# One PSUM tile shared out by the program, and seven column products in another order

## The chip, the cores and the metric

The kernel runs on one core of one Trainium2 chip. TensorE (PE in the profile, its weight loads PEld) multiplies, VectorE is DVE, ScalarE is ACT, GpSimd is POOL, and SyncE (SP) issues most DMAs. The metric is device time in microseconds (us) of one execution.

## The reference, cut to what matters

Two encoder layers on 256 tokens of width 2048, in float32:

```python
for l in range(2):
    h = rmsnorm(x, norm_mix[l])
    proj = einsum('bsd,de->bse', h, w_in[l])          # 2048 -> 3840
    ...                                               # three attention groups A, B, C
    x = x + einsum('bse,ed->bsd', mix, w_o[l])        # 2048 -> 2048
    h = rmsnorm(x, norm_mlp[l])
    u = relu(einsum('bsd,df->bsf', h, w_up[l]))       # 2048 -> 8192
    x = x + einsum('bsf,fd->bsd', u * u, w_down[l])   # 8192 -> 2048
return rmsnorm(x, norm_final)
```

## The kernel before

**Steps.** All matrix work is one list of `steps`, in the order in which TensorE takes them. A step has a weight piece of 128 x 1024 numbers. Its `split` writes the piece in two parts: ScalarE casts it (`whi`, L1023), then VectorE subtracts the cast from the piece (`wlo`, L1024). Its `mm` multiplies with both. `whi` and `wlo` have three buffers each, so the split of a step needs the buffers of the step three before it. The loop at the end of the program calls, for each step i, `load` for the steps up to seven ahead, `split` for the steps up to two ahead, then the `prep` of coming steps within their `look`, then `mm` of step i. A scheduler lays these calls out on the engines, and each engine then works strictly in its order.

**Up steps.** A quarter of a 256-column strip of `w_up` (L682, L687: 8 products of 512 columns with `whi`, 8 of 256 with `wlo`). After each fourth, `evac` squares the activations and forms sums of them: ScalarE copies a half (L660), VectorE adds the other (L661), ScalarE applies ReLU and squares (L662, L663), VectorE forms sums (L699 to L701), ScalarE and VectorE split the result (L668, L669).

**Strassen steps.** The down projection of a group g of 1024 hidden columns and a pair of 512-column blocks takes seven products P1 to P7 in place of eight. Each has two halves, here a and b, so a pair has 14 steps of 6 products (L802). Their weights come from the pieces B11, B12, B21, B22 of `w_down`:

- P1 uses B11, which is loaded into a `spare` tile, one for each half.
- When P1's split is done, a DMA that POOL issues (`on_top`, L786) adds B12 onto the B11 tile.
- P6 uses B22 + (B11 + B12): VectorE adds them (`sum_of`, L782) into a `big` tile, which is then split. P5 uses (B11 + B12) itself.
- P7 uses B12 + B22, which VectorE adds (L782); for the b half of the second pair of a group POOL's DMA adds it.
- P4 uses P6's sum, with B21 added by another DMA of POOL. P3 uses B22.

P1, P6, P5 and P3 are summed in one PSUM bank ("a"), P7 and P4 in the other ("d"), and P2 has a bank of its own. Both banks belong to one tile `S`. After the b half of P1, P6, P5, P3, P7 and P4 VectorE adds the bank to the residual x (`residual`, L225), while the next product in that bank goes on from the sum that stands there.

**Order.** `plan` gives the order of the products, and the `take` patterns mix them with up steps (0 an up step, 1 a Strassen step). In group 0 to 5 of each layer, two pairs (28 steps) are mixed with 16 up steps. This is called a round here; a layer has six. Group 6 alternates the two kinds, and group 7 has steps of a plain down projection between its products.

**PSUM.** Eight banks of 512 columns: two `pair` tiles of two banks (projections and up steps), two `tr` tiles of one bank (transposes, attention, P2) and the tile `S` (attention scores, then P1 to P7). A pool hands them out in turn.

Of the kernel before, what the change touches and what calls it, by code (L numbers as in the profile page):

```python
# [23 lines left out]
P = 128  # L24
# [19 lines left out]
def tile_trunk(ctx: ExitStack, tc: tile.TileContext, x_in, xt_in, w_in, w_o, w_up, w_down,  # L44
# [39 lines left out]

    def mm_pair():
        return pp.tile([P, 2, 512], F32, tag="pair", bufs=2, name=nm("mm"))

    def mm_banks():
        two = mm_pair()
        return [two[:, 0, :], two[:, 1, :]]  # L90

    def tr_bank():
        return pp.tile([P, 512], F32, tag="tr", bufs=2, name=nm("tr"))

    def score_banks():
        return pp.tile([P, 4, 256], F32, tag="S", bufs=1, name=nm("S"))
# [47 lines left out]
    def setup_avec():  # L144
# [8 lines left out]
        def mm():  # L153
# [3 lines left out]
            nc.sync.dma_start(avec, avs)  # L157
        add(mm, cost=0.9, delay=15.0)
# [68 lines left out]
    def hprep(key, gcol, j, hT, ss, done, fin_rs):  # L227

        def p(h):
# [6 lines left out]
            operand_pair(key, gcol, 2 * j + h, ps, hT)  # L236
            flags.add((done, 2 * j + h))
# [23 lines left out]
    def q_transposes(src, pr0, qT, scale):  # L261
# [10 lines left out]
        for par in range(2):  # L272
            lo, hi = 64 * par, 64 * par + 64
            nc.vector.scalar_tensor_tensor(qT[64:128, par::2, :], psr[lo:hi, :, :], scale, f(qT[0:64, par::2, :]),
                                           op0=ALU.mult, op1=ALU.subtract)

    def k_transposes(src, pr0, npr, kh, kl):
# [13 lines left out]
        nc.sync.dma_start(f(kl[64:128]), f(kl[0:64]))  # L291

# [92 lines left out]
    def unit_transp(u):  # L385
        u.ph = big(F32R, 2, 512)
        u.pl = big(F32R, 2, 512)
        for kb in range(2):
# [5 lines left out]
            nc.vector.tensor_sub(u.pl[:, kb, :], ps, f(u.ph[:, kb, :]))  # L394

    def unit_pv(u):
# [19 lines left out]
        for par in range(2):  # L416
# [4 lines left out]
            else:  # L421
                pv = ps.rearrange("p (h c) -> p h c", h=4)
                ov = ot.rearrange("p (h c) -> p h c", h=4)
                nc.vector.tensor_add(raw[rows, :, u.qb * P:(u.qb + 1) * P], pv[0:64, par::2, :], ov[:, par::2, :])
        if u.last:
            add(lambda: u.finish(raw), 0.0, delay=2.6, front=True)
# [28 lines left out]
    def mix_rs(l, grp, acc, done):  # L455
        ps = tr_bank()
        for t in range(NT):
# [3 lines left out]
                                1.0 / (256 * len(GROUP_BLOCKS[grp])), EPS, op0=ALU.mult, op1=ALU.add)  # L461
        done["r" + grp] = rsqrt(ms, 2)
# [5 lines left out]
    class Step:  # L468


        def __init__(self, src, kk, n, pre, mm, fourth=True, loads=None, prep=None, raw=None,
# [3 lines left out]
            self.loads, self.prep, self.raw = loads or [], prep, raw  # L475

# [30 lines left out]
    def layer_steps(l):  # L507
# [88 lines left out]
        for name in IN_CHUNKS:  # L596
# [5 lines left out]
            for k in range(nst):  # L602
# [6 lines left out]
                def mm(wh, wl, k=k, nk=nk, nst=nst, n=n, box=box, name=name):  # L609
                    if k == 0:  # L610
                        box["b"] = mm_banks()
                    hts = [of(halves(st["hT"][(k * nk + i) // 2])) for i in range(nk)]
                    mode_b(box["b"], hts, wh, wl, [(k * nk + i) % 2 for i in range(nk)], k == 0, k == nst - 1, n,
                           lo_last=l == 0 and name == IN_CHUNKS[0], by_block=k == 0)
                    if k == nst - 1:
                        proj_evac(name, box["b"])
# [5 lines left out]
        for grp in OUT_ORDER:  # L622
            blks = GROUP_BLOCKS[grp]
            for j in range(4):
                box = {}
                for bi, blk in enumerate(blks):
# [6 lines left out]
                    def mm(wh, wl, grp=grp, j=j, bi=bi, blk=blk, nb=len(blks), box=box):  # L633
                        if bi == 0:
                            box["b"] = mm_banks()
                        mode_b(box["b"], [of(st["mixT"][blk])] * 2, wh, wl, [0, 1], bi == 0, bi == nb - 1)
                        if bi == nb - 1:
                            need(("mixr", l, grp))
                            r = st["rg"]["r" + grp]
                            for t in range(NT):  # L640
                                xs = x[:, t, j * 512:(j + 1) * 512]
                                nc.vector.scalar_tensor_tensor(xs, box["b"][t], r[:, t:t + 1], xs,
                                                               op0=ALU.mult, op1=ALU.add)
# [575 lines left out]
```

## Time and profile before

| | |
|---|---|
| median of 3 runs | 2032.65 us (2029.82 to 2036.92) |
| profiled execution, whole | 2038.54 us |
| its span on the core | 2036.6 us |
| mean granted TensorE clock | 0.996 |
| VectorE busy | 1670.5 us (82% of the span) |
| ScalarE busy | 1291.1 us (63%) |
| POOL busy | 395.7 us (19%) |

The span is what the profile shows of the execution, from its first to its last instruction. Busy time is an average over stages: attention and projections fill the stretches up to about 324 us and from about 1008 to 1332 us, and the up and down projections the rest.

### The profile page before, as it was taken

To read this page: it belongs to the slowest core of one execution; us is meant where nothing else is said; L and a number is where in the kernel's file an instruction comes from. 1 tells how busy PE (TensorE), PEld (TensorE's weight loads), DVE (VectorE), ACT (ScalarE), POOL (GpSimd) and SP (SyncE) were. 2 spreads that over 40 slices of the span, in tenths; PEclk is the share of its full clock that TensorE was granted. 3 is DMA by queue.
4 is the path that set the end of the run, shared out by engine and by line. 5 is a ranking of instruction groups with operands and counts; after the bars stand their busy time and mean duration, and the time that the engine had idled before them with its cause. 6 is when DMAs were issued, how large, how long until landed. Compare 5 with 4: busy or idle time off the path is not lost.

```text
span 2036.6 us, 28114 instructions
## 1 busy us (share of the span) xinstructions
PE 1991.8 (98%) x10054; PEld 1668.7 (82%) x10054; DVE 1670.5 (82%) x2043; ACT 1291.1 (63%) x1750; POOL 395.7 (19%) x456
## 2 busy tenths in 40 slices
PE   9999999999999999999999999999999999999998
PEld 7888888888878888788888788888878888887887
DVE  6677877889888888988857678778888888988887
ACT  6657746666666666566656677566656666666664
POOL 0575520001010010100007655100010000101000
PEclk9999999999999999999999999999999999999999
DMA  8745655789898987887766465558788988989774
GB/s 329 209 145 163 199 174 187 228 239 260 238 249 251 270 232 242 252 245 220 218 187 194 145 184 186 174 189 241 236 247 238 267 238 240 260 244 242 238 223 156
DMA packets 127479, 452.08 MB, mean 222 GB/s; under 512 B 14531, under 2 KB 16835, under 8 KB 127340
## 3 DMA queue, kind: packets, MB, share of 16 engines
q1 hardware_dynamic: 109052, 384.18, 54.9%
q0 software_dynamic: 17856, 65.02, 19.3%
q8 instruction: 79, 1.29, 0.3%
q10 hardware_dynamic: 432, 1.10, 0.1%
q14 instruction: 60, 0.49, 0.1%
HBM read 444.45 MB, written 2.11 MB: 219 GB/s over the span
## 4 chain that ended last, share of the span: by engine, by line
PE 68%; issue 11%; DVE 9%; DMA 9%; ACT 3%; SPq 0%; POOL 0%; DVEq 0%; POOLq 0%; ACTq 0%
PE mm L483 26%; PE S L802 15%; PE mm L682 14%; PE mm L687 7%; DMA spare<-in_w_down_dram 6%; DVE wlo L1024 5%; PE tr L802 2%; ACT whi L1023 2%; DVE big L782 1%; PE tr L392 1%; DMA side<-in_w_down_dram 1%; DMA wraw<-in_w_in_dram 1%; PE tr L411 1%; PE S L354 1%; PE S L355 1%
## 5 line engine op out<-in xcount | busy, mean ns | idle before, releaser
L1024 DVE TENSOR_TENSOR wlo<-wraw,whi 128x1024 fp32r<-128x1024 f32 (+1 forms) x481 | 590.9, 1233 | 150.9 <-ACT whi L1023 138.8
L1023 ACT CAST whi<-wraw 128x1024 fp32r<-128x1024 f32 (+1 forms) x481 | 503.1, 1047 | 227.1 <-PE mm L483 72.2
L682 PE MATMUL mm<-big,whi 128*128 128x512 f32 x2048 | 516.7, 392 | 0.1
L682 PEld LDWEIGHTS mm<-big,whi 128*128 128x128 f32 x2048 | 379.4, 188 | 85.0 <-ACT whi L1023 8.0
L483 PE MATMUL mm<-whi,big 128*128 128x512 f32 (+1 forms) x1404 | 426.0, 387 | 0.9 <-DVE x L225 0.7
L802 PE MATMUL S<-whi,big 128*128 128x512 f32 x1344 | 373.5, 400 | 25.4 <-DVE x L225 22.2
L483 PEld LDWEIGHTS mm<-whi,big 128*128 128x128 f32 x1404 | 261.6, 190 | 49.9 <-ACT whi L1023 1.2
L687 PEld LDWEIGHTS mm<-big,wlo 128*128 128x128 f32 x2048 | 283.5, 190 | 22.6
L802 PEld LDWEIGHTS S<-whi,big 128*128 128x128 f32 x1344 | 235.5, 190 | 77.7 <-DVE x L225 22.2
L687 PE MATMUL mm<-big,wlo 128*128 128x256 f32 x2048 | 291.3, 282 | 0.0
L483 PE MATMUL mm<-wlo,big 128*128 128x512 f32 (+1 forms) x702 | 255.6, 384 | 0.0
L1023 ACT CAST whi<-big 128x1024 fp32r<-128x1024 f32 x112 | 117.6, 1050 | 170.0 <-DVE big L782 112.5
L802 PE MATMUL S<-wlo,big 128*128 128x512 f32 x672 | 210.3, 394 | 0.7
L1023 ACT CAST whi<-side 128x1024 fp32r<-128x1024 f32 x112 | 117.5, 1049 | 140.4 <-DVE side L782 115.3
L786 POOL DMA_DIRECT2D spare<-in_w_down_dram x56 | 48.9, 873 | 715.9 <-DVE wlo L1024 705.4
L1024 DVE TENSOR_TENSOR wlo<-big,whi 128x1024 fp32r<-128x1024 f32 x112 | 136.7, 1221 | 37.0 <-ACT whi L1023 36.9
L1024 DVE TENSOR_TENSOR wlo<-spare,whi 128x1024 fp32r<-128x1024 f32 x112 | 136.6, 1220 | 34.0 <-ACT whi L1023 33.9
L1024 DVE TENSOR_TENSOR wlo<-side,whi 128x1024 fp32r<-128x1024 f32 x112 | 136.7, 1221 | 32.6 <-ACT whi L1023 29.5
L802 PEld LDWEIGHTS S<-wlo,big 128*128 128x128 f32 x672 | 125.6, 189 | 33.7 <-DVE wlo L1024 6.4
L483 PEld LDWEIGHTS mm<-wlo,big 128*128 128x128 f32 x702 | 133.8, 191 | 23.6 <-DVE wlo L1024 0.2
L1023 ACT CAST whi<-spare 128x1024 fp32r<-128x1024 f32 x112 | 117.2, 1047 | 46.1 <-PE S L802 19.5
L483 PE MATMUL mm<-spare,big 128*128 128x512 f32 (+1 forms) x606 | 142.4, 382 | 0.0
(154 smaller groups left out, 2216.7 us busy)
## 6 DMA issues: line engine op xcount, KB each, us to landing
wraw<-in_w_up_dram SPq DMA_DIRECT2D x256, 512.0 KB, 5.3
wraw<-in_w_in_dram SPq DMA_DIRECT2D x119, 512.0 KB, 3.7
side<-in_w_down_dram SPq DMA_DIRECT2D x112, 512.0 KB, 4.9
wraw<-in_w_down_dram SPq DMA_DIRECT2D x88, 512.0 KB, 5.5
wraw<-in_w_o_dram SPq DMA_DIRECT2D x64, 512.0 KB, 3.7
spare<-in_w_down_dram SPq DMA_DIRECT2D x56, 512.0 KB, 6.3
spare<-in_w_down_dram POOLq DMA_DIRECT2D x56, 512.0 KB, 8.3
big<-in_w_down_dram POOLq DMA_DIRECT2D x56, 512.0 KB, 7.3
```

The lines of the kernel that those rows point to most:

```text
L354: nc.tensor.matmul(o, st, u.kh[:, kh, :], start=True, stop=False)
L355: nc.tensor.matmul(o, st, u.kl[:, kh, :], start=False, stop=True)
L392: nc.tensor.transpose(ps[:, c * P:(c + 1) * P], u.p[:, s, kb * P:(kb + 1) * P], ident)
L411: nc.tensor.matmul(ps, u.V[:, kb, u.kv, :, :], pt[:, kb, :], start=n == 0, stop=n == 3)
L483: nc.tensor.matmul(banks[t][:, 0:n], a, (wl if part == "hl" else wh)[:, i, :], start=first and i == 0 and part == "hh", stop=last and i == ...
L682: nc.tensor.matmul(box["b"][:, fs, :], wh[:, kk, fs * P:(fs + 1) * P], ht, start=s == 0 and kk == 0, stop=False, skip_group_check=True)
L687: nc.tensor.matmul(box["b"][:, fs, 0:256], wl[:, kk, fs * P:(fs + 1) * P], ht[:, 0:256], start=False, stop=s == 3 and kk == 3, skip_group_ ...
L782: nc.vector.tensor_add(to, a, b)
L786: nc.gpsimd.dma_start(tile, src(par, j, h).rearrange("p (k n) -> p k n", k=2), accum_op=ALU.add)
L802: nc.tensor.matmul(o, ops[i][a], w[:, i, :], skip_group_check=True, start=fresh and h == 0 and i == 0 and a == 0 and w is wh and (bk != "b ...
L1023: last_act[0] = nc.scalar.copy(h[:, part], w[:, part]).ins
L1024: last_lo[0] = nc.vector.tensor_sub(lo[:, part], w[:, part], f(h[:, part])).ins
```

## The change

Three things change.

1. PSUM is one tile `psum` of eight banks. `mm_pair` takes the pair of free banks that was freed longest ago among banks 0 to 5, `tr_bank` a single one, and `release` gives them back at the place in the program where the last reader was issued. The tile `S` becomes banks 6 and 7.
2. The order of the products is P1 P2 P6 P7 P5 P4 P3 instead of P1 P2 P7 P6 P5 P3 P4. The two halves of P1 and P2 come first (P1a P2a P1b P2b), and the others follow half by half. Banks "a" and "d" now alternate (P6 a, P7 d, P5 a, P4 d, P3 a), and swap roles from pair to pair (`flip`). The load of B22 moves from P7 to P6.
3. The mix is 18 up steps first (16 before), then `11011011010` four times in each round, and in group 6 `10` 14 times.

```diff
+    psum = pp.tile([P, 8, 512], F32, name="psum")
+    live, freed, turn = {}, [0] * 6, [0]
     def mm_pair():
-        return pp.tile([P, 2, 512], F32, tag="pair", bufs=2, name=nm("mm"))
+        n = min((p for p in range(3) if not {2 * p, 2 * p + 1} & set(live)), key=lambda p: max(freed[2 * p:2 * p + 2]))
+        two = psum[:, 2 * n:2 * n + 2, :]
+        live[2 * n] = live[2 * n + 1] = two
+        return two
     def tr_bank():
-        return pp.tile([P, 512], F32, tag="tr", bufs=2, name=nm("tr"))
+        n = min((b for b in range(6) if b not in live), key=lambda b: ((b ^ 1) not in live, freed[b]))
+        live[n] = psum[:, n, :]
+        return live[n]
+    def release(*banks):
+        for b in [b for b in live if any(live[b] is o for o in banks)]:
+            del live[b]
+            turn[0] += 1
+            freed[b] = turn[0]
     def score_banks():
-        return pp.tile([P, 4, 256], F32, tag="S", bufs=1, name=nm("S"))
+        return psum[:, 6:8, :].rearrange("p a (b c) -> p (a b) c", b=2)
...
-                    ("P7", "S3", "d", True, (1, 1, -1)), ("P6", "S2", "a", False, (1, 0, 1)),
-                    ("P5", "S1", "a", False, (1, 1, -1)), ("P3", "S4", "a", False, (0, 1, -1)),
-                    ("P4", "A22", "d", False, (1, 0, 1))]
+                    ("P6", "S2", "a", False, (1, 0, 1)), ("P7", "S3", "d", True, (1, 1, -1)),
+                    ("P5", "S1", "a", False, (1, 1, -1)), ("P4", "A22", "d", False, (1, 0, 1)),
+                    ("P3", "S4", "a", False, (0, 1, -1))]
...
-            first, then = [(p_, h) for h in range(2) for p_ in plan[:3]], [(p_, h) for p_ in plan[3:] for h in range(2)]
+            first, then = [(p_, h) for h in range(2) for p_ in plan[:2]], [(p_, h) for p_ in plan[2:] for h in range(2)]
+            flip = turns[0] % 2
+            turns[0] += 1
...
-                    if "S" not in keep:
-                        keep["S"] = score_banks().rearrange("p (b i) n -> p b (i n)", i=2)
-                    box["a"], box["d"] = keep["S"][:, 0], keep["S"][:, 1]
+                    box["a"], box["d"] = psum[:, 6 + flip, :], psum[:, 7 - flip, :]
...
                 elif name == "P7":
-                    loads = [(("B22", h), src(1, 1, h), None)]
...
                 elif name == "P6":
+                    loads = [(("B22", h), src(1, 1, h), None)]
...
-        take("0" * 16, ups)
+        take("0" * 18, ups)
         for g in range(6):
-            take("11010" + "110" * 10 + "10" * 3 + "011", ups, strassen_steps(g) + strassen_steps(g, 1))
-        take("00" + "1010" * 6 + "1010", ups, strassen_steps(6))
+            take("11011011010" * 4, ups, strassen_steps(g) + strassen_steps(g, 1))
+        take("10" * 14, ups, strassen_steps(6))
```

The lines left out call `release` behind the last reader of a bank. Two places show how the engines' orders move, both in the first pair of group 1 of the first layer.

The first is VectorE from the split of P1b to the split of P6b. Before, the rows are: the splits of P1b, P2b and an up step, the sum for P7b (`side`), the sum for P6a (`big`), P1 to the residual, the splits of P7b, P6a and an up step, the sum for P6b, P7 to the residual, and the split of P6b.

```order
L1024 TENSOR_TENSOR wlo_873_4523<-spare_858_4459,whi_872_4522 128x1024 [waits DMAHW5_49,PE_49,Activation_49]
L1024 TENSOR_TENSOR wlo_876_4536<-wraw_862_4474,whi_875_4535 128x1024 [waits DMAHW2_49,PE_49,Activation_49]
L1024 TENSOR_TENSOR wlo_878_4556<-wraw_865_4487,whi_877_4555 128x1024 [waits DMAHW3_49,PE_49,Activation_49]
L782 TENSOR_TENSOR side_861_4472<-side_861_4472,side_868_4499 128x1024 [waits DMAHW7_49,DMAHW1_49]
L782 TENSOR_TENSOR big_879_4560<-side_849_4412,spare_839_4353 128x1024 [waits DMASW1_49]
L225 SCALAR_TENSOR_TENSOR x_78<-S_722_3730,rsq_83,x_78 128x512 [waits PE_49]
L1024 TENSOR_TENSOR wlo_881_4570<-side_861_4472,whi_880_4569 128x1024 [waits Activation_49]
L1024 TENSOR_TENSOR wlo_884_4582<-big_879_4560,whi_883_4581 128x1024 [waits PE_49,Activation_49]
L1024 TENSOR_TENSOR wlo_886_4603<-wraw_874_4533,whi_885_4602 128x1024 [waits DMAHW4_49,PE_49,Activation_49]
L782 TENSOR_TENSOR big_887_4606<-side_868_4499,spare_858_4459 128x1024 [waits DMASW2_49]
L225 SCALAR_TENSOR_TENSOR x_78<-S_722_3730,rsq_83,x_78 128x512 [waits PE_49]
L1024 TENSOR_TENSOR wlo_889_4616<-big_887_4606,whi_888_4615 128x1024 [waits Activation_49]
```

In the changed program VectorE has, at the same place, the splits of P1b and P2b, the sum for P6a, the split of an up step, P1 to the residual, the split of P6a, the sum for P6b and its split, then the split of the next up step, the addition for the squares of the strip that ended, and the sum for P7a.

```order
L1050 TENSOR_TENSOR wlo_753_4414<-spare_738_4339,whi_752_4413 128x1024 [waits DMAHW0_49,PE_49,Activation_49]
L1050 TENSOR_TENSOR wlo_756_4427<-wraw_742_4363,whi_755_4426 128x1024 [waits DMAHW1_49,PE_49,Activation_49]
L806 TENSOR_TENSOR big_757_4430<-side_748_4399,spare_725_4278 128x1024 [waits DMAHW2_49,DMASW1_49]
L1050 TENSOR_TENSOR wlo_759_4449<-wraw_745_4377,whi_758_4448 128x1024 [waits DMAHW3_49,PE_49,Activation_49]
L236 SCALAR_TENSOR_TENSOR x_79<-psum_72,rsq_84,x_79 128x512 [waits PE_49]
L1050 TENSOR_TENSOR wlo_762_4462<-big_757_4430,whi_761_4461 128x1024 [waits Activation_49]
L806 TENSOR_TENSOR big_763_4465<-side_751_4411,spare_738_4339 128x1024 [waits DMAHW4_49,DMASW2_49]
L1050 TENSOR_TENSOR wlo_765_4474<-big_763_4465,whi_764_4473 128x1024 [waits PE_49,Activation_49]
L1050 TENSOR_TENSOR wlo_770_4507<-wraw_754_4424,whi_769_4506 128x1024 [waits DMAHW5_49,PE_49,Activation_49]
L683 TENSOR_TENSOR wide_766_4494<-wide_766_4494,psum_72 128x512 [waits Activation_49]
L806 TENSOR_TENSOR side_731_4312<-side_731_4312,side_748_4399 128x1024
```

Between the split of P1b (first row), behind which the DMA adds B12 onto the tile, and the sum for P6b that reads this tile, eight instructions stood before and five stand now. On TensorE four Strassen and two up steps lay from the start of P1b to that of P6b before, and three and one lie there now.

The second place is TensorE, a little later, at the first up step behind P6b; its products begin a new strip. Before, its rows with P6b's last product ahead are these, with the pair `mm_893` other than that of the strip before (`mm_871`).

```order
L802 MATMUL S_722_3730<-wlo_889_4616,big_829_4305 128x512 [waits DVE_49]
L802 MATMUL S_722_3730<-wlo_889_4616,big_853_4442 128x512
L682 MATMUL mm_903_4687<-big_612_3135,whi_896_4660 128x512 [waits Activation_49]
L682 MATMUL mm_903_4687<-big_612_3135,whi_896_4660 128x512 x3
L682 MATMUL mm_903_4687<-big_614_3145,whi_896_4660 128x512 x4
```

In the changed program the same place reads so.

```order
L826 MATMUL psum_72<-wlo_765_4474,big_699_4131 128x512 [waits DVE_49]
L826 MATMUL psum_72<-wlo_765_4474,big_729_4308 128x512
L705 MATMUL psum_72<-big_512_3036,whi_769_4506 128x512 [waits DVE_49]
L705 MATMUL psum_72<-big_512_3036,whi_769_4506 128x512 x3
L705 MATMUL psum_72<-big_513_3045,whi_769_4506 128x512 x4
```

The first product of the strip waited for ScalarE's cast before, and waits for VectorE now, for the addition in the last row but one above (L683), which reads the bank pair of the strip ahead. The strip takes the same pair again: bank 0 is held by the warm-up products at the program's start (`wb`, which nothing releases), and in the rounds P2 of the first pair holds bank 1 and P2 of the second a bank of another pair, so that one whole pair is left. Before, strips took two `pair` tiles in turn.

40 lines of the change are left out of this document (26 added, 14 removed).

## The prediction

> **What bounds the kernel now.** I read the page first: busy shares, then the waits of TensorE, then windows over the rounds, then the timeline of one pair.
>
> ```profile
> span 2036.6 us, 28114 instructions
> PE 1991.8 (98%) x10054; PEld 1668.7 (82%) x10054; DVE 1670.5 (82%) x2043; ACT 1291.1 (63%) x1750; POOL 395.7 (19%) x456
> ```
>
> TensorE is the bound, and its work is the same after the change: same products, same shapes. Only its waits can change. The list of waits names the one that matters:
>
> ```profile
> PE S L802 <- DVE x L225: 22.2, 22, 2.0
> ...
> PE tr L283 <- DVE big L394: 1.9, 2, 0.9
> PE tr L267 <- DVE avs L156: 1.8, 1, 1.8
> ```
>
> The columns are total us, times and longest. Strassen products wait 22 times for a bank to be added to the residual. Windows laid on a round (first row, group 1 of layer 0) and on group 6, where up and Strassen steps alternate (second row), show where:
>
> ```profile
> 456.50:542.70 86.20, 84.71 (x425) 70.49 (x424) 76.46 (x84) 54.98 (x61) 7.85 (x9) 1.00 0.86 250
> ...
> 895.90:959.50 63.60, 63.60 (x334) 54.74 (x333) 54.56 (x60) 42.00 (x47) 3.49 (x4) 1.00 0.80 235
> ```
>
> After the length come busy PE, PEld, DVE, ACT, POOL, the granted clock, DMA share and GB/s. TensorE idles in the round and not in group 6. VectorE is busy 76.46 of 86.20 us, so it is the second bound, with some 10 us to spare in a round.
>
> Busy PE hides part of a stall, because ends are modelled. So I count by starts. TensorE alone:
>
> ```profile
> 708.55 1.98 PE L682 MATMUL mm<-big,whi 128*128 128x512 f32 x8
> 710.36 1.11 PE L687 MATMUL mm<-big,wlo 128*128 128x256 f32 x8
> 711.32 2.00 PE L682 MATMUL mm<-big,whi 128*128 128x512 f32 x8
> 713.16 1.12 PE L687 MATMUL mm<-big,wlo 128*128 128x256 f32 x8
> 714.11 1.09 PE L802 MATMUL S<-whi,big 128*128 128x512 f32 x4
> 715.04 0.62 PE L802 MATMUL S<-wlo,big 128*128 128x512 f32 x2
> 715.50 1.07 PE L802 MATMUL S<-whi,big 128*128 128x512 f32 x4
> ```
>
> An up step takes 2.78 us (708.55 to 711.32, to 714.11), a Strassen step 1.38 us (714.11 to 715.50), of which 0.93 before its `wlo` products. A round without a wait is 28 x 1.38 + 16 x 2.78 = **83.1 us**. What it is shows POOL's first DMA of a round, four rounds apart:
>
> ```profile
> 455.62 0.88 POOL L786 DMA_DIRECT2D spare<-in_w_down_dram  x1 [20.91 <-DVE wlo L1024]
> ...
> 802.17 0.87 POOL L786 DMA_DIRECT2D spare<-in_w_down_dram  x1 [20.92 <-DVE wlo L1024]
> ```
>
> (802.17 - 455.62) / 4 = **86.6 us**, so 3.5 us of waits in a round. With 12 rounds that is 42 us, all that a better order can win there.
>
> One pair of that round, from the split of P1b on:
>
> ```profile
> 464.94 1.22 DVE L1024 TENSOR_TENSOR wlo<-spare,whi 128x1024 fp32r<-128x1024 f32 x1
> ...
> 466.45 0.87 POOL L786 DMA_DIRECT2D spare<-in_w_down_dram  x1 [9.95 <-DVE wlo L1024]
> ...
> 470.61 0.74 DVE L225 SCALAR_TENSOR_TENSOR x<-S,rsq,x 128x512 f32<-128x512 f32 x1
> ...
> 474.68 1.22 DVE L782 TENSOR_TENSOR big<-side,spare 128x1024 f32<-128x1024 f32 x1
> ...
> 475.81 0.74 DVE L225 SCALAR_TENSOR_TENSOR x<-S,rsq,x 128x512 f32<-128x512 f32 x1
> 476.01 1.05 ACT L1023 CAST whi<-big 128x1024 fp32r<-128x1024 f32 x1 [3.20 <-DVE big L782]
> 476.61 1.20 PE L802 MATMUL S<-whi,big 128*128 128x512 f32 x4 [0.40 <-DVE x L225]
> ...
> 479.36 0.68 DVE L661 TENSOR_TENSOR wide<-wide,mm 128x512 f32<-128x512 f32 x1
> ...
> 480.28 0.72 ACT L662 ACTIVATE wide<-wide,zero 128x512 f32<-128x512 f32 x1
> 481.04 0.72 ACT L663 ACTIVATE wide<-wide,zero 128x512 f32<-128x512 f32 x1
> ...
> 481.67 1.04 ACT L1023 CAST whi<-side 128x1024 fp32r<-128x1024 f32 x1
> ...
> 483.09 0.62 PE L802 MATMUL S<-wlo,big 128*128 128x512 f32 x2
> ...
> 483.29 1.05 ACT L1023 CAST whi<-wraw 128x1024 fp32r<-128x1024 f32 x1 [0.58 <-PE S L802]
> ```
>
> P6a (476.61) waits for P7b's read (475.81 to 476.55), though P7 sums in the other bank of `S` and P1's read of P6a's own bank ended at 471.35. Two banks in one tile are held as one. And the DMA of 466.45 feeds the sum of 474.68, the cast of 476.01 and P6b, nearly without slack. Its time:
>
> ```profile
> DMA to landing us min/median/max: 5.2/7.9/9.8
> ```
>
> (answer on POOL's DMA line, 124 of them).
>
> **The change part by part.** *Bank waits.* P6a now waits for P1's read alone, with P2b and an up step (4.2 us) between. The other products follow a product in the other bank. I take the whole 42 us of waits out of the rounds and add below what comes in. [...]
>
> *The DMA ahead of P6b.* P1b's split needs the buffers of P1a, three steps earlier. Counted from P1a's start: 0.93 to the end of its `whi` products, 0.20 until the cast starts (483.09 to 483.29), 1.05 cast, 1.22 `wlo`, so 3.40 at the earliest. Then 0.29 to the issue (466.16 to 466.45), L to the landing, 1.22 for the sum, 0.11 to the cast, 1.05 cast: P6b starts no sooner than 6.07 + L. TensorE gets there after P1a P2a up P1b P2b up P6a, 5 x 1.38 + 2 x 2.78 = 12.46. L was 5.2 to 9.8; before, another up step and P7b lay between, so it hardly showed. I take the median 7.9, since about as many loads are in flight: P6b comes at 13.97, 1.5 late, and its `wlo` products 0.29 later still (1.22 against 0.93). **1.8 us a pair.** At 9.8 it is 3.7, at 6.4 only the 0.29.
>
> *The up step behind it.* P6b's cast ends when P6b starts. From there VectorE splits P6b (1.22) and an up step (1.13 back to back), and then adds for the squares (0.68); the next strip waits for this read, since it gets the same banks. With 0.06 to start (476.55 to 476.61) that is 3.1 us. TensorE has P6b alone ahead, 1.38 + 0.29 = 1.67. **1.4 us a pair**; at the strip's other change two Strassen steps lie ahead and VectorE is not late: nothing. Bounds: nothing, if VectorE is ahead there too, to 1.4. P7a, next, is then in time: VectorE's addition, ReLU (0.1 later), square 0.76 behind it, P7a's cast 0.63 behind that and 1.04 long (480.28, 481.04, 481.67) end 5.6 us after P6b's start, TensorE comes at 3.1 + 2.78 = 5.9.
>
> *P7b, first pair of a round.* Behind P7a's cast VectorE does its `wlo`, a short sum of the squares, the split of an up step, the split of the squares and the sum for P7b; then comes the cast.
>
> ```profile
> L669 DVE TENSOR_TENSOR big<-wide,big 128x896 fp32r<-128x896 f32 (+1 forms) x64 | 71.7, 1120 | 2.8 <-ACT big L668 2.6
> ...
> L701 DVE SCALAR_TENSOR_TENSOR wide<-wide 128x128 f32<-128x128 f32 x64 | 18.3, 287 | 0.8
> ```
>
> 1.22 + 0.29 + 1.13 + 1.12 + 1.22 + 0.11 + 1.05 = 6.1, so 11.7 us after P6b's start, against 5.9 + 1.38 + 2.78 = 10.1 on TensorE: **1.6 us**, once a round (in the second pair a DMA adds this sum). Bounds: 0 to 1.6.
>
> *The rest.* Behind P7b come P5, P4 and P3, whose weights are long there, so VectorE catches up: it has 76.5 us of work in a longer round. The even pattern I cost at nothing: a lone Strassen step gives TensorE 1.38 us and VectorE a split of 1.13, and the three buffers smooth the rest; without them the four sums of a pair would show. More banks for transposes should take away waits such as the two `tr` rows above, 3.7 us, taken as 4; the least is nothing. The two up steps moved ahead and P4 ahead of P3 at a layer's end cost nothing, as their work is the same.
>
> **Sum.** A round: 83.1 + 2 x 1.8 + 2 x 1.4 + 1.6 = 91.1 us, 4.5 more than before. 12 rounds: +54; transposes: -4; together **+50 us**. The profiled execution took 2038.54 us, 0.3% over the median of the runs, 2032.65; I add the difference to the median: **2083 us**. With L at 9.8: 3.8 a round more, 2128.
>
> **The rivals.** *Faster: the DMA lands early.* With L at 5.2, the sum for P6b starts at 8.9, its cast ends at 11.3 and P6b is in time. VectorE's addition ends at 11.3 + 3.1 = 14.4, TensorE comes to the strip at 12.46 + 1.38 = 13.84: 0.5. Round 83.1 + 1.0 + 1.6 = 85.7, 0.9 under before: -11 - 4, 2018 us. It decides at L of about 5.8, between this and L of 6.4 (83.1 + 0.6 + 2.8 + 1.6 = 88.1 a round, 14 us over before). For it: at 3.7 us P1b's DMA overlaps fewer loads of the next pair. Against: the row's median. [...]
>
> *No change: VectorE is ahead behind P6b.* Then only 1.8 a pair comes in, 83.1 + 3.6 = 86.7, as before, and 2029 us. Against it: in VectorE's order the addition stands behind P6b's split.
>
> *The one tile is held as one.* Then each product waits for the last read anywhere: at least the 0.40 of the row above (longest 2.0) for each of 12 reads in a round, 12 x 12 x 0.4 = 58 us on top, 2141. Against it: the code hands the banks out singly; no row of before shows a tile of eight.
>
> **How the numbers follow.** Late at P6b, the strip and P7b, L between about 6.9 and 9.8 (2058 to 2128): 0.62. Partly hidden or no change (2027 to 2057): 0.18. Faster (2018 and around): 0.14. Held as one, or worse: 0.06. Within 0.3%, about what a measurement of this kernel can tell from no change, is 2027 to 2039: 0.08 of the second case; the rest of it is slower. So faster 0.14, same 0.08, slower 0.78. The range leaves out the fast landing and the top: 2026 to 2118.
>
> **What would show it.** Right: no wait of P6a on L225 (or L236 as it is called then); waits of Strassen products for ScalarE's cast instead, at P6b and P7b, and of up steps for L683; rounds near 91 us; VectorE's sums idle for POOL's DMA (7.7 us in total before). Wrong: rounds under 86.6, or POOL's DMA landing at under 6 us at the median, or no wait of an up step for L683.

## The result: slower by 4.8%, and the profile after

| | before | after |
|---|---|---|
| median | 2034.65 us (4 runs, 2029.82 to 2036.92) | 2128.16 us (4 runs, 2120.05 to 2149.21) |
| ratio | | 1.0479 (95%: 1.0400 to 1.0557) |
| profiled execution, its span | 2038.54, 2036.6 us | 2127.17, 2125.3 us |
| mean granted TensorE clock | 0.996 | 0.981 |

The change costs 93.5 us. 2083 us were forecast, in a range of 2026 to 2118: the direction was right, the size was not. First the head of the page of the changed kernel:

```profile
span 2125.3 us, 28129 instructions
...
PE 2028.8 (95%) x10054; PEld 1680.3 (79%) x10054; DVE 1692.1 (80%) x2043; ACT 1304.8 (61%) x1750; POOL 394.7 (19%) x456
```

TensorE has as many products as before (10054), yet is busy 37 us longer: a part of its products ran slower, at a lower granted clock, and busy PE hides a part of its waits, because ends are modelled (in the round of before it was 84.71 of 86.20 us, where the products alone take 83.1). Most of the rest of the 88.7 us between the two spans is waiting. What its products waited for, from the list of waits (line waited for: total us, times, longest):

```profile
PE psum L826 <- ACT whi L1049: 51.1, 39, 2.8
PE psum L705 <- DVE wide L683: 15.4, 20, 1.0
PE psum L406 <- DVE big L408: 8.0, 12, 1.4
```

L826 are Strassen products and L1049 is the cast, L705 is an up step and L683 VectorE's addition, as forecast. No wait for the residual read (now L236) is left, where before there were 22. The last row is as good as new (before it was 0.4 us, twice): transposes of attention (L406) wait for VectorE's read (L408) of the bank they are to write. The same list for weight loads has it larger:

```profile
PEld psum L826 <- ACT whi L1049: 67.2, 51, 3.2
PEld psum L705 <- DVE wide L683: 26.8, 20, 1.4
PEld psum L406 <- DVE big L408: 16.9, 31, 1.8
```

Windows show where the time went. They run from the start to the first up step of layer 0, over the round of group 1, over group 6, and from group 7 of layer 0 to the first up step of layer 1. After:

```profile
0.00:332.33 332.33, 319.45 (x1573) 260.80 (x1573) 242.39 (x376) 211.41 (x387) 141.51 (x166) 0.99 0.61 196
475.25:570.55 95.30, 89.96 (x426) 74.48 (x425) 78.07 (x84) 56.22 (x61) 7.85 (x9) 0.93 0.81 226
940.85:1007.83 66.98, 65.10 (x334) 54.62 (x333) 54.14 (x60) 41.04 (x46) 3.50 (x4) 1.00 0.77 224
1007.83:1390.55 382.72, 373.88 (x1848) 306.08 (x1846) 282.83 (x390) 237.36 (x419) 143.44 (x163) 1.00 0.58 178
```

Before, the first and the last of these (the other two stand in the prediction):

```profile
0.00:324.24 324.24, 317.09 (x1581) 264.21 (x1581) 238.68 (x377) 210.88 (x388) 141.98 (x166) 0.99 0.63 201
959.53:1331.96 372.43, 369.08 (x1856) 308.78 (x1854) 279.52 (x391) 236.76 (x420) 143.95 (x163) 1.00 0.60 183
```

Three stages lose. Projections and attention lose 8.1 us in layer 0 and 10.3 on the way to layer 1; with 1.2 us in each stretch of up steps ahead of group 0 that is 21. Group 6 takes 66.98 us for 63.60, so 7 in two layers. The twelve rounds, from the first Strassen product of one to that of the next, sum to 1105 us, 61 more than before (without the two up steps that before had in group 5). Together, within rounding, that is the 88.7 us.

One pair of a round, the first of group 1, from P1b on:

```profile
476.64 1.07 PE L826 MATMUL psum<-whi,big 128*128 128x512 f32 x4
...
479.03 0.87 POOL L810 DMA_DIRECT2D spare<-in_w_down_dram  x1 [5.20 <-DVE wlo L1050]
...
486.28 1.09 PE L826 MATMUL psum<-whi,big 128*128 128x512 f32 x4
...
487.33 1.22 DVE L806 TENSOR_TENSOR big<-side,spare 128x1024 f32<-128x1024 f32 x1 [3.08 <-DMA spare<-in_w_down_dram]
488.66 1.04 ACT L1049 CAST whi<-big 128x1024 fp32r<-128x1024 f32 x1 [5.66 <-DVE big L806]
...
489.76 1.19 PE L826 MATMUL psum<-whi,big 128*128 128x512 f32 x4 [1.93 <-ACT whi L1049]
...
492.02 0.68 DVE L683 TENSOR_TENSOR wide<-wide,psum 128x512 f32<-128x512 f32 x1
...
492.75 3.78 PE L705 MATMUL psum<-big,whi 128*128 128x512 f32 x8 [0.61 <-DVE wide L683]
```

This is the chain of the prediction. P1b starts at 476.64; the DMA is issued at 479.03 and the sum that reads it starts at 487.33, 8.3 us later, after VectorE stood idle for 3.08. P6a starts at 486.28 and ends 1.38 later, but P6b starts only at 489.76, 2.1 us late. The up step behind it waits for L683. Over the whole program VectorE's sums stood idle for this transfer far longer than the 7.7 us of before:

```profile
DVE big L806 <- DMA spare<-in_w_down_dram: 63.9, 34, 3.7
```

What the prediction did not have is in the last row of the timeline: these eight products take 3.78 us, not the 1.98 of an up step. Windows of 2 us over the same place (the third number from the end of a row is the granted clock):

```profile
488.00:490.00 2.00, 0.24 (x1) 0.24 (x2) 0.81 (x2) 1.34 (x2) 0.00 (x0) 1.00 0.78 154
490.00:492.00 2.00, 1.94 (x6) 0.83 (x5) 2.00 (x2) 1.14 (x2) 0.74 (x1) 0.79 0.05 10
492.00:494.00 2.00, 1.39 (x4) 1.06 (x4) 2.00 (x4) 1.24 (x2) 0.13 (x1) 0.50 0.68 59
494.00:496.00 2.00, 2.00 (x6) 1.51 (x6) 1.94 (x4) 2.00 (x3) 0.00 (x0) 0.50 0.95 199
...
498.00:500.00 2.00, 2.00 (x11) 1.65 (x10) 1.89 (x2) 0.02 (x1) 0.00 (x0) 1.00 0.90 309
```

Behind the wait the clock is 0.50 for 6.8 us. Counted over the whole trace this happens 14 times between the first 60 us and the last 10 (one more than the expectation of e5 says), for 3.41 or 6.83 us each; before it happened once. The 3.41 us ahead of each of these stretches were not empty: they held four to eight products, 0.7 to 1.3 us of work at 0.227 us for one of 512 columns, and one wait of 2.0 to 3.0 us. In 12 of the 14 that wait is P6b's.

### The profile page after: what moved, and what is told of

It reads as the page before. It is cut to its first block, busy times and chain, and to the rows that moved or that the text cites. A ratio compares the mean times of both kernels' runs of the same rounds, so it can differ in the third digit from the quotient of the medians.

```text
span 2125.3 us, 28129 instructions
## 1 busy us (share of the span) xinstructions
PE 2028.8 (95%) x10054; PEld 1680.3 (79%) x10054; DVE 1692.1 (80%) x2043; ACT 1304.8 (61%) x1750; POOL 394.7 (19%) x456
## 5 line engine op out<-in xcount | busy, mean ns | idle before, releaser
L1049 ACT CAST whi<-wraw 128x1024 fp32r<-128x1024 f32 (+1 forms) x481 | 503.7, 1047 | 312.8 <-PE psum L705 121.6
L705 PE MATMUL psum<-big,whi 128*128 128x512 f32 x2048 | 530.8, 401 | 15.4 <-DVE wide L683 15.4
L826 PE MATMUL psum<-whi,big 128*128 128x512 f32 x1568 | 431.8, 397 | 51.4 <-ACT whi L1049 51.1
L705 PEld LDWEIGHTS psum<-big,whi 128*128 128x128 f32 x2048 | 390.5, 193 | 109.5 <-DVE wide L683 26.8
L503 PE MATMUL psum<-whi,big 128*128 128x512 f32 (+1 forms) x1404 | 429.1, 388 | 0.3 <-ACT whi L1049 0.3
L826 PEld LDWEIGHTS psum<-whi,big 128*128 128x128 f32 x1568 | 278.4, 190 | 112.0 <-ACT whi L1049 67.2
L710 PEld LDWEIGHTS psum<-big,wlo 128*128 128x128 f32 x2048 | 286.0, 194 | 21.0
L503 PEld LDWEIGHTS psum<-whi,big 128*128 128x128 f32 x1404 | 261.8, 191 | 50.3 <-ACT whi L1049 2.8
L710 PE MATMUL psum<-big,wlo 128*128 128x256 f32 x2048 | 292.3, 286 | 0.0
L503 PE MATMUL psum<-wlo,big 128*128 128x512 f32 (+1 forms) x702 | 257.2, 387 | 0.0
L826 PE MATMUL psum<-wlo,big 128*128 128x512 f32 x784 | 250.6, 401 | 1.0
L1049 ACT CAST whi<-big 128x1024 fp32r<-128x1024 f32 x112 | 117.8, 1051 | 195.7 <-DVE big L806 134.1
L826 PEld LDWEIGHTS psum<-wlo,big 128*128 128x128 f32 x784 | 146.8, 191 | 42.4 <-DVE wlo L1050 12.0
L1050 DVE TENSOR_TENSOR wlo<-big,whi 128x1024 fp32r<-128x1024 f32 x112 | 136.5, 1219 | 35.7 <-ACT whi L1049 34.1
L1049 ACT CAST whi<-side 128x1024 fp32r<-128x1024 f32 x112 | 117.3, 1047 | 68.0 <-DVE side L806 31.3
L503 PEld LDWEIGHTS psum<-wlo,big 128*128 128x128 f32 x702 | 133.8, 191 | 23.2 <-DVE wlo L1050 0.3
L1049 ACT CAST whi<-spare 128x1024 fp32r<-128x1024 f32 x112 | 117.6, 1050 | 49.8 <-PE psum L826 29.4
```

The lines of the kernel that those rows point to most:

```text
L503: nc.tensor.matmul(banks[t][:, 0:n], a, (wl if part == "hl" else wh)[:, i, :], start=first and i == 0 and part == "hh", stop=last and i == ...
L705: nc.tensor.matmul(box["b"][:, fs, :], wh[:, kk, fs * P:(fs + 1) * P], ht, start=s == 0 and kk == 0, stop=False, skip_group_check=True)
L710: nc.tensor.matmul(box["b"][:, fs, 0:256], wl[:, kk, fs * P:(fs + 1) * P], ht[:, 0:256], start=False, stop=s == 3 and kk == 3, skip_group_ ...
L826: nc.tensor.matmul(o, ops[i][a], w[:, i, :], skip_group_check=True, start=fresh and h == 0 and i == 0 and a == 0 and w is wh and (bk != "b ...
L1049: last_act[0] = nc.scalar.copy(h[:, part], w[:, part]).ins
L1050: last_lo[0] = nc.vector.tensor_sub(lo[:, part], w[:, part], f(h[:, part])).ins
```

## The experiments

Each batch of runs (e1 to e4, e5 to e8, e9 to e11, e12) ran on one chip together with the kernel before, whose median was 2030 to 2034 us. Differences between runs of two batches can be off by as much as these medians are, some 4 us. Counts "by starts" sum, over the products of a kind of step, the time from one start to the next less that of an undisturbed product (0.227 us at 512 columns, 0.119 at 256: in the prediction's rows of TensorE alone, eight take 1.81 and 0.95 us). They go over all 28 pairs of the two layers where "in the rounds" is not said. What products lost that started at a clock of 0.50 is counted apart.

**e1: the warm-up bank handed back.** Both kernels begin with eight products on zeros, the warm-up, into a bank `wb`. In the changed one nobody releases it.

```diff
     for _ in range(N_WARM):
         nc.tensor.matmul(wb, warm[:, 0:P], warm, start=True, stop=True)
+    release(wb)
```

> The changed kernel with one line more: the bank of the warm-up products is handed back behind them, so that six banks are free for pairs and transposes and not five. Theory A (the 93.5 us come from three waits, two of them for banks): P2 of the two column pairs then sits in the two banks of one pair, up steps have two pairs, the 20 waits of up steps for VectorE's addition (L683, 15.4 us on the matmuls, 26.8 on the weight loads) go, and so do the transposes' waits for L408 (8.0 and 16.9 us); the waits of P6b for the cast stay. Some 45 + 17 us less: about 2065 us, granted clock back to 0.99. Theory B (VectorE is simply late in this order, the bank only names it): within 10 us of 2128, and the waits move to another line. Theory C (the clock is lower because of the order alone): waits go but the clock stays at 0.98.

Measured: 2077.07 us (2070.87 to 2083.04), clock 0.992. The waits for L683 and L408 are gone. The windows from the start and to layer 1, and the round of group 1:

```profile
0.00:315.02 315.02, 311.55 (x1581) 262.69 (x1581) 239.38 (x378) 211.03 (x388) 137.54 (x166) 1.00 0.64 207
457.49:547.38 89.89, 84.86 (x427) 70.50 (x426) 77.52 (x84) 55.72 (x61) 7.86 (x9) 1.00 0.85 240
...
979.10:1347.88 368.78, 366.97 (x1855) 309.69 (x1854) 280.60 (x392) 236.93 (x420) 139.51 (x163) 1.00 0.60 185
```

17.3 and 13.9 us come back ahead of the up steps of the two layers. That is more than the change had lost there, so the new PSUM is better for these stages than the old one once this bank is free. The rounds gain only 11 us in all. By starts, in the rounds, the waits of up steps fall from 22 us to 1, but those of P7a and P7b rise from 13 to 33 and those of P6b from 52 to 56: together the waits stay as long, and what is won is that products slowed by the clock fall from 26 us to 13. Theory A holds ahead of the rounds, and B in the rounds: nearly all that the up steps had waited comes back at other products.

**e2 and e3: the new PSUM in the old order.** Plan and patterns undone, banks without swapped roles; e3 also with `release(wb)`.

```diff
-            plan = [..., ("P6", "S2", "a", ...), ("P7", "S3", "d", ...), ..., ("P4", ...), ("P3", ...)]
+            plan = [..., ("P7", "S3", "d", ...), ("P6", "S2", "a", ...), ..., ("P3", ...), ("P4", ...)]
-            take("11011011010" * 4, ups, strassen_steps(g) + strassen_steps(g, 1))
+            take("11010" + "110" * 10 + "10" * 3 + "011", ups, strassen_steps(g) + strassen_steps(g, 1))
```

> PSUM as one tile shared out by the program, with the order of before (plan and patterns undone, banks without swapped roles), warm-up bank still kept. Theory A: the 22 waits of P6a for the residual read (22.2 us on the page, some 32 us counted by starts) go, transposes lose 17 us as in the changed kernel, strips lose little since VectorE is not late in this order: 2010 to 2035 us. Rival D (the new PSUM handling is what costs, the order is harmless): 2080 us or more, with up steps waiting for L683.

> As e2, with the warm-up bank handed back. Theory A: only the gain is left: no wait for the residual read, none of transposes: 1995 to 2010 us, faster than both kernels. Rival (VectorE, busy 76.46 of 86.20 us in a round, takes over as the bound when P6a no longer waits): 2025 us or more, with the waits at the splits instead.

Measured: e2 2042.68 us (2040.14 to 2043.15), 8 us above the band; e3 2010.02 (2007.66 to 2012.78), ratio 0.9901 (0.9886 to 0.9915), at the edge of its own. With the bank handed back the new PSUM wins 20 us over before, and the kept bank costs 33 us. The two kernels' windows ahead of the up steps of the two layers, e2 first:

```profile
0.00:332.37 332.37, 319.39 (x1573) 260.59 (x1573) 242.44 (x376) 211.47 (x387) 141.45 (x166) 0.99 0.62 196
...
961.74:1343.37 381.63, 373.21 (x1848) 306.28 (x1846) 283.26 (x390) 237.51 (x419) 143.44 (x163) 1.00 0.59 179
```

```profile
0.00:315.59 315.59, 311.44 (x1580) 262.16 (x1581) 239.32 (x378) 211.11 (x388) 137.52 (x166) 1.00 0.64 207
...
943.86:1311.78 367.92, 366.46 (x1855) 309.91 (x1854) 280.62 (x392) 237.08 (x420) 139.51 (x163) 1.00 0.60 185
```

16.8 + 13.7 us lie in these two, 2.3 in the up steps ahead of group 0, and the rounds of the two kernels are of one length in sum (1038 us for e2, 1039 for e3, with the two up steps that stand in group 5). So the kept bank takes its 33 us outside the rounds here, in the stages with transposes, though in e2 too up steps wait 20 times for L683. The rule of `tr_bank` would explain it: by the code it prefers a bank whose neighbour is taken, and the neighbour of the kept bank 0 is always taken, so transposes get bank 1 again and again and wait for its last read (31 times in the list of weight loads of e2, as in the changed kernel). No run changes this rule alone.

**e4: the order on the old PSUM.** Plan, patterns and swapped roles of the change, with the pools of before.

```diff
-                    box["a"], box["d"] = keep["S"][:, 0], keep["S"][:, 1]
+                    box["a"], box["d"] = keep["S"][:, flip], keep["S"][:, 1 - flip]
```

> The new order, patterns and swapped roles on the PSUM pools of before, where the two banks of S are one tile. Theory A: P6b waits for the cast as in the changed kernel (about 50 us), P7b 13; up steps and transposes do not wait for banks; the P6a waits of before go, but three products of a pair (P5a, P4a, P3a) follow a product of the other bank directly and wait some 0.8 us for its read: 24 x 3 x 0.8 = 58 us. About 2034.65 - 32 + 50 + 13 + 58 = 2124 us (2095 to 2150). Rival D (the order is harmless, PSUM costs): within 20 us of 2035.

Measured: 2108.28 us (2106.95 to 2111.57), inside the band, but for another reason: the waits at P5a, P4a and P3a that I had priced at 58 us are nearly gone (6 us by starts). From P7b (first row) to P5a (last row), which are neighbours in the plan:

```profile
489.96 1.19 PE L804 MATMUL S<-whi,big 128*128 128x512 f32 x4 [1.45 <-ACT whi L1026]
...
491.86 2.11 PE L682 MATMUL mm<-big,whi 128*128 128x512 f32 x8
493.81 0.76 PE L687 MATMUL mm<-big,wlo 128*128 128x256 f32 x5
494.40 1.09 PE L804 MATMUL S<-whi,big 128*128 128x512 f32 x4
```

The scheduler has put 13 of the 16 products of an up step between them (six to nine ahead of P4a and P3a), and they cover the read. P6b has 48 us by starts, P7a and P7b 44. So the order alone costs 78 us, and a tile held as one little in this order, laid out like this.

**e5: filling the wait.** Six products of the warm-up operand behind P6a, while TensorE waits for P6b.

```diff
+                    if (name, h) == ("P6", 1):
+                        with tc.issue_after(box["last"]):    # the last product of P6a
+                            for _ in range(6):
+                                nc.tensor.matmul(wb, warm[:, 0:P], warm, start=True, stop=True)
```

> The changed kernel, with six products of the warm-up operand (1.4 us of TensorE) put behind P6a, into the wait ahead of each P6b, 28 times; they write the warm-up's own bank and nothing reads it. In the changed kernel's trace the granted clock is 0.50 for 3.41 or 6.83 us each time little work was done just before, 13 times between the start and the end, mostly behind P6b and a waiting up step; products started there cost some 26 us more in the rounds than at full clock. Theory E (idle time itself lowers the clock, and that was the missing term): the same waits, more work for TensorE, and yet faster: about 2102 us (2090 to 2112), clock 0.99. Rival F (the low clock goes with something else, and idle time is only beside it): 2128 to 2145 us, clock 0.98.

Measured: 2115.73 us (2113.24 to 2117.98), clock 0.997: 168 products more, and 12 us less. The place of the timeline above, in its own round:

```profile
487.77 1.54 PE L826 MATMUL psum<-warm 128*128 128x512 f32 x6
489.30 1.19 PE L830 MATMUL psum<-whi,big 128*128 128x512 f32 x4
...
492.30 2.14 PE L705 MATMUL psum<-big,whi 128*128 128x512 f32 x8 [1.00 <-DVE wide L683]
```

The wait for L683 is still there, but the up step behind it takes 2.14 us and not 3.78. Theory E is right in kind: with products in the waits the mean clock is 0.997, where it was 0.981. The price of the low clock is some 12 us and not 26. (The ratios to before, 1.0479 with 1.0400 to 1.0557 and 1.0402 with 1.0386 to 1.0417, leave that open by a few us; by the two traces the rounds are 11 us shorter.) By starts, in the rounds, 26 us of slowed products disappear, but the time before P6b (filled or waiting) grows by 4 and the waits of P7 and the up steps by 10: TensorE comes there sooner and waits for VectorE instead. A round has 91.2 us now, against 92.1 with the low clock.

**e6: B11 + B12 by VectorE, on e1.**

```diff
-                        on_top(raw["B11", h], 0, 1, h)
+                        sum_of(raw["B11", h], raw["B11", h], raw["B12", h])
```

> The kernel of e1 (warm-up bank freed, 2077 us), with B11 + B12 added by VectorE from the loaded B12 in place of POOL's DMA: one sum of 1.22 us more for each of 56 halves, 68 us of VectorE's work, and no DMA between the split of P1b and P6b. Theory A (P6b waits because this DMA lands late): P6b's wait (56 us by starts) goes, VectorE has 4.9 us more in a round of 91 us and is near its limit, P7 stays late: 2025 to 2055 us. Rival G (P6b is late for the order of casts and splits, the DMA is only the last in the list): 2070 us or more.

Measured: 2045.88 us (2044.87 to 2046.79), 31 less than e1. P6b falls from 56 to 21 us by starts, P7a and P7b rise from 37 to 46. The DMA was the larger part of P6b's wait; behind it stands VectorE's own chain, which has one sum more here, and all rounds take between 87.7 and 88.3 us.

**e7: the even pattern with the old plan, on e3.** Only the `take` patterns of the change.

> The kernel of e3 (new PSUM with the warm-up bank freed, old plan, 2010 us), with the even pattern of up and Strassen steps. P7 still lies between P1 and P6, so P6b stays six Strassen steps and two or three up steps behind P1a. Theory A (P6's place in the plan costs, the pattern does not): 2000 to 2020 us. Rival H (the even pattern uses up the buffers' slack by itself): 2045 us or more, with waits for the cast at P7 or P6.

Measured: 2060.04 us (2055.23 to 2060.69), 50 above e3: rival H, but not by its reason. P6b alone waits, 63 us by starts, and VectorE's list of waits has no row for a DMA. From the end of the up step ahead of P6b to P6b, in one pair:

```profile
477.87 1.11 PE L710 MATMUL psum<-big,wlo 128*128 128x256 f32 x8
478.37 1.09 DVE L692 TENSOR_TENSOR big<-wide,big 128x896 fp32r<-128x896 f32 x1 [1.06 <-ACT big L691]
479.38 1.22 DVE L806 TENSOR_TENSOR big<-side,spare 128x1024 f32<-128x1024 f32 x1
480.68 1.04 ACT L1048 CAST whi<-big 128x1024 fp32r<-128x1024 f32 x1 [2.35 <-DVE big L806]
...
481.78 0.50 PE L826 MATMUL psum<-whi,big 128*128 128x512 f32 x1 [2.80 <-ACT whi L1048]
```

The sum for P6b (479.38) stands behind the split of an up strip's squares (L692), which had waited for ScalarE, and TensorE idles 2.80 us. It is so in all 24 pairs of the rounds: a split of squares that idled 1.1 or 1.2 us stands directly ahead of the sum for P6b. In this plan the even pattern brings the end of a strip to just this place.

**e8: an up step ahead of P6b, on e1.**

```diff
-            take("11011011010" * 4, ...)
+            take(("11011010110" + "11011011010") * 2, ...)
```

> The kernel of e1, with the up step behind P6b put ahead of it (between P6a and P6b): the only move. Theory A (P6b comes 2.3 us too early for the DMA): TensorE has 2.78 us more, P6b's wait (56 us) falls under 15; the waits of P7a and P7b (37 us) may stay: 2025 to 2050 us. Rival G (the whole chain of VectorE behind it shifts): the wait moves to P7a and P7b, 2065 us or more.

Measured: 2039.79 us (2038.46 to 2047.81), 37 less than e1. P6b's wait falls from 56 to 5 us by starts; P7a's rises from 17 to 37, P7b's falls from 20 to 13. Theory A holds: one digit of the pattern decides P6b. A quarter of what that saves comes back at P7.

**e9: the sums for P7 by POOL's DMA, on e8.**

```diff
-                    by_dma = (pair, h) == (1, 1)
+                    by_dma = True
```

> The kernel of e8 (2040 us), with all four sums for P7 of a round made by POOL's DMA, as before only P7b of the second pair: three sums of 1.22 us less for VectorE in a round, three DMAs of 512 KB more. Theory J (P7 waits, 50 us by starts in e8, because its sums stand in VectorE's order behind the sums for P6 and the splits): P7's waits fall under 15 us, 2000 to 2015 us. Rival K (the DMA lands no earlier than VectorE would be done, at a DMA share of 0.85 already): P7 goes on waiting, or P6b waits again since its own DMA lands later: 2030 us or more.

Measured: 1983.31 us (1981.44 to 1984.02), ratio 0.9758 (0.9744 to 0.9773): faster than the kernel before by 49 us, and the fastest of all. Its head, a round and group 6:

```profile
PE 1964.0 (99%) x10054; PEld 1670.0 (84%) x10054; DVE 1634.9 (83%) x1999; ACT 1304.8 (66%) x1750; POOL 424.1 (21%) x500
```

```profile
450.48:533.25 82.77, 82.77 (x426) 70.86 (x425) 74.39 (x81) 56.08 (x61) 10.36 (x12) 1.00 0.96 280
866.88:932.50 65.62, 64.23 (x334) 54.65 (x333) 51.99 (x58) 41.37 (x46) 5.18 (x6) 1.00 0.82 244
```

TensorE idles nowhere in the round, although DMA share is 0.96. The rounds take 82.8 to 83.5 us. So what held P7 were VectorE's sums for it: those for P6a, P6b, P7a and P7b come one behind the other, each with a split of an up step between. Whether their place in this order or their 1.22 us each counts, e9 does not separate.

**e10 and e11: the same on e3.** e10 has `by_dma = True` as above; e11 only the b halves:

```diff
-                    by_dma = (pair, h) == (1, 1)
+                    by_dma = h == 1
```

> The kernel of e3 (old plan and patterns, new PSUM, warm-up bank freed, 2010 us), with the sums for P7 made by POOL's DMA. Theory J (what is left in the rounds, some 2.5 us each over 83.1, is VectorE's: P6a and P6b wait for casts behind sums): 1990 to 2003 us. Rival K (more DMA delays the other DMAs): 2010 us or more, with sums idle for POOL's DMA.

> The kernel of e3, with the sums for P7b of both pairs made by POOL's DMA, P7a by VectorE: one sum less for VectorE in a round. Theory J: between e3 and e10, 2000 to 2010 us. Rival K: as e3 or slower.

Measured: e10 2038.93 us (2029.56 to 2043.25), e11 2013.43 (2007.27 to 2018.71). In the old order it does not help, and with all four it costs 29 us: VectorE's sums for P6 idle 45.8 us for POOL's DMA, 14 times, up to 4.6. Theory J is wrong there. The traces show what differs from e9. In e10 the DMA behind P1b lands 10.1 us after its issue at the median (8.3 in e3), and in 15 of 28 pairs, where a DMA for P7 and one for P4 are on their way at the same time, 11.0. In e9 no DMA for P7 overlaps with one behind P1, and the latter take 6.5 behind P1b. That this overlap is the cause was not tried.

**e12: e9 with the warm-up bank kept.**

```diff
-    release(wb)
```

> The kernel of e9 (1983 us), with the warm-up bank kept as in the changed kernel. In e2 and e3, which differ in this bank alone, the rounds are of one length, and the 32.7 us between them all lie in projections and attention. Theory L (in a round the missing bank costs nothing, waits of up steps for it only name a lateness that is there anyway): 2016 us (2010 to 2022), rounds near 83 us. Rival M (in the new order, where an up step stands right behind P6b or P6a, the wait for the bank is a cost of its own, 22 us by starts in the changed kernel): 2030 us or more, rounds near 85.

Measured: 2038.98 us (2030.08 to 2043.95), 56 above e9. From its list of waits:

```profile
PE psum L705 <- DVE wide L683: 16.6, 15, 2.1
```

35.7 us of it lie ahead of group 0 of the two layers, and the rounds are 22 us longer in sum. Rival M: in the new order the up step's wait for the bank is a cost of its own where nothing else is late.

## Why the prediction was right, and where it was wrong

Its sum over the twelve rounds, and what the changed kernel shows by starts, all in us:

| term | forecast | shown |
|---|---|---|
| P6b behind the DMA | 43 | 51.7 |
| up step behind P6b | 34 | 22 |
| P7b, first pair | 19 | 13 (P7b 10.7, P7a 2.5) |
| waits of the old rounds that go | -42 | -47 |
| low clock | not there | 26 (12 net, e5) |
| outside the rounds: group 6 | 0 | 7 |
| transposes, projections, attention | -4 | +21 |

The counts by starts hold a few us that are not waits: with the -47 the rows of the rounds come to 66 us, where the rounds of the two kernels differ by 61.

**TensorE alone, 83.1 us a round.** Right: e9, where nothing waits, has 82.8 to 83.5.

**Bank waits of P6a.** Right: its waits on the residual read fell from 22 to none. But the 42 us that I took for them were all the waits of the old rounds, and over all twelve these were 47: the old rounds sum to 1044 us, less 12 x 83.1. The 3.5 us a round came from four rounds of layer 0. In the old order, where the bank waits alone go (e3), the rounds win only 16 us, since casts and splits are late next (its list of waits has Strassen products behind casts 15 times, 4.8 us).

**P6b.** The mechanism is right (P6b's 56 us by starts in e1 fall to 21 in e6 and to 5 in e8, in two ways), the size was low: 2.15 us a pair for 1.8. The term that was off is L. The median of 7.9 was over all of POOL's DMAs; for the b halves of `spare` the time from the issue to the sum's start is 8.4 at the median in the changed kernel. 6.07 + 8.4 - 12.46 is 2.0 late, and 0.29 more for `wlo`. On the page all 56 `spare` DMAs together have 7.2, so a median over both halves would have misled as well. The two halves differ, and did so before: from the issue to landing the b halves took 8.8 us at the median in the kernel before, the a halves 5.6. The answer on POOL's DMA line after the change, all 124 of them:

```profile
DMA to landing us min/median/max: 5.3/6.9/9.7
```

**The up step behind P6b.** Right in its mechanism, 1.1 us for each of the 20 or so and not 1.4. e1 shows that with the bank free nearly all of it reappears at P7 and P6b; e12 that it costs by itself where those do not wait (22 us in the rounds). (A step of its working is misread, without effect: in the rows shown ReLU starts 0.24 us behind the addition's end, at 480.28, and not 0.1.)

**P7.** About right in the changed kernel, but I took it as small. It was hidden behind the other two waits: 37 us in e1, 50 in e8, over all pairs.

**The failed step** is the sentence on the transposes: "More banks for transposes should take away waits such as the two `tr` rows above, 3.7 us, taken as 4; the least is nothing." In its place the runs show 21 us lost, since there was not more but less: the kept bank and the preference for its neighbour left one bank in turn (the preference by the code, not by a run). From 4 us won to 21 lost are 25 us, most of the 39 by which the difference of the two spans, 88.7, exceeds the forecast 50; group 6 and the rounds make 7 each. With the bank handed back (e3) the same stages win 13 us over before. The prediction knew that few banks were left for up steps, and did not ask the same of transposes. Its "least is nothing" also closed the range from the wrong side.

**Two smaller ones.** "The even pattern I cost at nothing" rested on the three buffers, "without them the four sums of a pair would show". They do show in group 6, which loses 3.4 us in each layer with the new plan (e1, e4 and e6 too) and none with the old one (e7). VectorE there, in e1, from the split of a strip's squares ahead of the sum for P6a to the sum for P6b:

```profile
926.53 1.23 DVE L692 TENSOR_TENSOR big<-wide,big 128x1024 fp32r<-128x1024 f32 x1 [1.17 <-ACT big L691]
927.67 1.22 DVE L806 TENSOR_TENSOR big<-side,spare 128x1024 f32<-128x1024 f32 x1
930.06 1.23 DVE L1050 TENSOR_TENSOR wlo<-big,whi 128x1024 fp32r<-128x1024 f32 x1 [1.17 <-ACT whi L1049]
931.20 1.22 DVE L1050 TENSOR_TENSOR wlo<-wraw,whi 128x1024 fp32r<-128x1024 f32 x1
932.33 1.22 DVE L806 TENSOR_TENSOR big<-side,spare 128x1024 f32<-128x1024 f32 x1
```

Sum, cast and two splits take 4.66 us, and TensorE comes round in 1.38 + 2.78 = 4.16, so each sum behind the first comes some 0.5 later. P6a, the first, is 1.4 late already by starts: its sum stands behind the split of squares, as P6b's does in e7. The other: no term was there for the clock, which was 0.50 for 3.41 or 6.83 us behind 14 waits of 2.0 to 3.0 us. At a clock of 0.997 (e5) a round takes 91.2 us, where 91.1 were forecast; that is luck, because P6b was put too low and the up step and P7 too high. And it is chance that the measured 2128 us is the prediction's figure for L at 9.8: L was 8.4, and most of what was missing lay outside the rounds.

**The rivals.** "The DMA lands early" fell with the medians (6.9 of all, 8.4 for the b halves; it needed 5.8). "VectorE is ahead behind P6b" fell with the 20 waits for L683. "The one tile is held as one" fell with P6a, whose wait for the other bank is gone, and with e3.

## What to carry to other kernels

When a program takes over the handing out of buffers, list who never gives one back and what the choosing rule then does, for every user of the pool and not only for the one in view. A product that needs a transfer must be placed by the time that this transfer's own kind takes, not by a median over all of them: here 8.4 us at the median, where 7.9 was taken. Where several operands in a row need a sum on one engine, count the cycle of sum, cast and split against TensorE's time between them: here one moved up step and three sums given to a DMA turned 47 us of loss (e1) into 49 of gain (e9).

## What was not expected of the hardware

The clock falls to 0.50 for 3.41 us or twice that though TensorE is not idle for as long in these places: in the changed kernel one wait of 2.0 to 3.0 us lay ahead of each of the 14 stretches. Of the 16 waits at P6b of 2 us or more in the rounds of the changed kernel, 12 were followed by it. In each trace all stretches at 0.50 start on one grid of 3.41 us (in those of before and after to within 4 ns), and the four waits without consequence lie across a border of this grid with 0.6 us or more on each side; of the other twelve none has more than 0.4 us on its smaller side. Counted in windows of the grid at full clock, through the rounds and group 6 of all fourteen traces, 0.50 followed in 44 of 45 windows with up to 1.30 us of product work (0.227 us for 512 columns, 0.119 for 256), in 8 of 19 with 1.30 to 1.41, and in none of some 4,650 with more. In the traces of before and after alone, from 60 us on to 14 us before the end, it followed in all 15 with up to 1.30 us, in none of the 7 with 1.36, and in none of the 1,129 with more. With 168 products that compute nothing in the waits (e5) the mean clock was 0.997 for 0.981, and the kernel was some 12 us faster.

More DMA need not slow the DMA that P6b needs: in e9, with a DMA share of 0.96 in a round for 0.81, the `spare` ones land in 6.4 us at the median, where the changed kernel has 7.2. In e10, in the old order, it did slow the one behind P1b, from 8.3 to 10.1. The page of e9:

```profile
spare<-in_w_down_dram POOLq DMA_DIRECT2D x56, 512.0 KB, 6.4
```
